# Two recurrences woven into an attention: the recurrence is handed out evenly up to the attention's last step instead of ending two steps ahead of it

## The chip, the cores and the metric

The kernel runs on one core of a Trainium2 chip. The metric is the device time of one execution in microseconds (us), less is better; several executions give a median. Beside the times there is one execution taken by the hardware profiler, with its trace. TensorE (PE) multiplies matrices, PEld is its loading of weights, VectorE (DVE), ScalarE (ACT) and GpSimd (POOL) do the rest of the arithmetic, and SyncE (SP) issues nearly all DMA transfers from one queue, in order.

## The reference

A trunk of two layers over 256 context rows and 2048 latent rows of width 1024, in float32. Each layer projects its input, runs two gated linear recurrences in both directions and one attention, and projects the three results together:

```python
h = layer_norm(x) * (1.0 + scale) + shift
(hq, hff, hfb, hi, hgate, mcq, mckv, mkr, mgate, gq, gk, gv, gaf, gab, ggate) = split_cols(h @ w_in)
...
hg_lat, hg_ctx = bidirectional_recurrence(hgrn2_inputs(...), ...)
gla_lat, gla_ctx = bidirectional_recurrence(gla_inputs(...), ...)
mla_lat = blockwise_attend(q, jnp.concatenate([k_c, k], axis=1), jnp.concatenate([v_c, v], axis=1))
y = jnp.concatenate([gated_head_norm(hg_lat, hg_norm_g, hgate),
                     mla_lat.reshape(B, N, MLA_W) * jax.nn.silu(mgate),
                     gated_head_norm(gla_lat, gla_norm_g, ggate)], axis=-1)
x_new = layer_norm(DEEPNORM_ALPHA * x + gate * (y @ w_out)) * ln_g + ln_b
```

The attention has 4 heads; every latent row looks at all 2304 rows. The recurrence, S_t = diag(exp(g_t)) S_(t-1) + k_t v_t and o_t = q_t S_t, is computed in chunks of 64 rows. The context rows run through everything in the first layer only.

## The kernel before, in words

A layer has three stages, one behind the other in the code: `project`, `mix` and `output`. Numbers are split into a high and a low part (`split`, lines 75 to 85: ScalarE rounds the high part at L79, VectorE subtracts at L85, or GpSimd at L83), and each product is three products of parts.

**The mixing stage, `mix`.** The attention works through groups of two tiles of 128 query rows. A tile has two steps, one for each pair of heads; so a group has four steps, and layer 1 has 8 groups and 32 steps. Layer 0 has 36, since a context group stands at the third place, whose steps see only the context. A step (`attend`) makes scores (`pss`, L905 to L909), scaled by VectorE into `sx` (L911), takes their maximum, lets ScalarE take the exponential in place (L924), transposes it on TensorE (`ptp`, L951), splits it into `ph` and `pl` (L79, L85), multiplies it with the compressed keys (`oc`, L938 and L943), copies that (`os`, L967), multiplies it with `uv` (`poa`, L970), and scales and gates it (`ym`, L974). Behind a tile's second step the rows `ym` are stored to `y` (L977); the gate's rows `mg` come by L892.

The recurrence works in 9 pairs of tiles. First come the states of the backward direction (`back_states`, one part for each pair, 1.0 units each), then for each pair ten parts of 0.25 units (`recur`): 31.5 units in all. A pair ends with `chunk_outputs`: products `po` on TensorE (L807, L818), `o` and its squares on ScalarE (L822, L825), their sums on VectorE (L827), a root and two multiplications on GpSimd (L90, L831, L832), and the store of `o` to `y` (L833).

Both are generators, and `mix` weaves them: before each attention step it writes as many parts of the recurrence as are due.

```python
total = self.npairs * 3.5
cost = [(self.CHEAP if t == 0 else 1.0) for t in order for _ in range(4)]
end = max(sum(cost) - self.LEAD, 1.0)
done, spent = 0.0, 0.0
for c in cost:
    spent += c
    while done < spent * total / end:
        ...
        done += w
    next(att, None)
```

With `LEAD` 2 the last part of the recurrence is written ahead of the last two steps. The order in the code is the priority of the instructions; a scheduler fixes from it, when the kernel is built, the order of the instructions of each engine and of SyncE's queue, and on the chip each runs in that order.

**The output stage, `output`.** Its tiles lie in memory that the pools of the mixing stage free. It loads the gate (L1058) and then w_out in eight pieces of 512 KB (`woraw`, L1066), each split into two `wo` (L79 and L83 for even pieces, L79 and L85 for odd ones); `lng` and `lnb` follow (L1073, L1074). The pieces have the tag "yt" with two buffers, and the same two buffers then hold the rows of `y` (`yt`, L1078). A tile of rows is transposed (`pty`, L1085), split into `yhl`, multiplied (`pzo`, L1105 to L1107), and then gated, added to the rows `xto` (L1098), normalized and stored (L1127) on the way over `z`.

**The next layer's weights.** While layer 0 ends, SyncE also loads the first input weights of layer 1 (`wraw`, L355, with three buffers; `wh` and `wl` are their split) and its `uv` (L260); they have a high priority.

Of the kernel before, what the change touches and what calls it, by code (L numbers as in the profile page):

```python
# [54 lines left out]
class Trunk:  # L55
# [923 lines left out]
    def mix(self, l, S):  # L979

        nc = self.nc
        with ExitStack() as ctx:
# [46 lines left out]
# [3 lines that stand above are left out]
# [96 lines left out]

    AHEAD = 600
    SOON = 300  # L1130
    LEAD = 2
    WHEN = 2
    CHEAP = 0.3
    EARLY = 1000
# [95 lines left out]
```

## Time and profile before

| | us |
|---|---|
| median of 2 runs | 3741.56 (3741.3 to 3741.82) |
| profiled execution, its own time | 3734.03 |
| its span in the trace | 3732.1 |
| PE busy in the span | 3597.6 (96%) |
| DVE, ACT, POOL busy | 2135.8, 1502.0, 810.8 |

The span runs from the first to the last instruction in the trace; the execution's own time has a little around it. Layer 0's mixing stage ends near 1722 us of the span and layer 1's near 3541. An engine counts as busy while it works on an instruction. An instruction's idle time before it is put down to the event that came last, its releaser.

### The profile page before, as it was taken

Reading aid. Unit: us, or ns where it says so; the run is one execution under the profiler, and the core shown is the slowest. Engines: PE = TensorE matmul, PEld = TensorE weight load, DVE = VectorE, ACT = ScalarE, POOL = GpSimd, SP = SyncE. Lnnn points to the kernel's source line nnn. Section 1 sums busy time; section 2 is a strip of 40 time slices with the busy share of each in tenths; the row PEclk is TensorE's granted clock in tenths of the full one; section 3 lists DMA queues with packets and bytes.
Section 4 is the critical chain, followed back from the end, with each engine's and each line's share of the span. In section 5 each row is a group of like instructions: output and inputs, shape, how many; then the busy total and the mean of one; then the engine's idle time right before and its main releaser. Section 6 shows DMA issues by size and latency. Waiting matters only on the chain. (4 is left out here: it accounts for less than half of the span.)

```text
span 3732.1 us, 85224 instructions
## 1 busy us (share of the span) xinstructions
PE 3597.6 (96%) x36056; PEld 3253.3 (87%) x36056; DVE 2135.8 (57%) x5162; ACT 1502.0 (40%) x2808; POOL 810.8 (22%) x617
## 2 busy tenths in 40 slices
PE   8899999999999999999999999999999999999899
PEld 5899999888888888887879999997888888888787
DVE  6764242466666666666765442425665566566566
ACT  3525242344454544453115252523444444544400
POOL 1000000001246454441110000000022344644211
PEclk9999999999999999999999999999999999999999
DMA  7774444322122122116435443533231122221332
GB/s 257 231 205 146 127 132 145 112 72 96 48 65 87 62 65 71 47 53 212 156 107 169 147 148 119 159 107 118 76 94 39 61 68 62 70 84 41 103 144 102
DMA packets 263693, 410.84 MB, mean 110 GB/s; under 512 B 39632, under 2 KB 179984, under 8 KB 262288
## 3 DMA queue, kind: packets, MB, share of 16 engines
q1 hardware_dynamic: 261872, 403.04, 33.9%
q8 instruction: 283, 4.64, 0.5%
q10 hardware_dynamic: 1440, 2.36, 0.2%
q14 instruction: 98, 0.80, 0.1%
HBM read 288.66 MB, written 116.67 MB: 109 GB/s over the span
## 5 line engine op out<-in xcount | busy, mean ns | idle before, releaser
L421 PE MATMUL pj<-wh,hl 128*128 128x256 f32 (+1 forms) x2224 | 622.1, 280 | 8.2 <-DVE hl L85 8.2
L421 PE MATMUL pj<-wh,hh 128*128 128x256 f32 (+1 forms) x2224 | 623.7, 281 | 1.6 <-DVE ve L373 1.4
L421 PE MATMUL pj<-wl,hh 128*128 128x256 f32 (+1 forms) x2224 | 622.7, 280 | 0.0
L911 DVE TENSOR_SCALAR_CACHE_REDUCE sx<-pss 128x512 f32<-128x512 f32 (+1 forms) x648 | 401.9, 631 | 199.9 <-PE pss L909 167.2
L85 DVE TENSOR_TENSOR pl<-ptp,ph 128x512 fp32r<-128x512 f32 x580 | 389.8, 687 | 154.2 <-ACT ph L79 146.6
L79 ACT CAST ph<-ptp 128x512 fp32r<-128x512 f32 x580 | 326.1, 584 | 292.0 <-PE ptp L951 273.4
L421 PEld LDWEIGHTS pj<-wh,hl 128*128 128x128 f32 x2224 | 420.0, 189 | 8.9 <-DVE hl L85 8.9
L421 PEld LDWEIGHTS pj<-wh,hh 128*128 128x128 f32 x2224 | 420.9, 189 | 2.0 <-DVE ve L373 1.6
L421 PEld LDWEIGHTS pj<-wl,hh 128*128 128x128 f32 x2224 | 420.8, 189 | 0.0
L924 ACT ACTIVATE sx<-sx,nm 128x768 f32<-128x768 f32 (+1 forms) x392 | 359.5, 920 | 147.5 <-DVE nm L917 145.9
L951 PE MATMUL ptp<-ident,sx 128*128 128x128 f32 x2320 | 365.6, 276 | 19.8 <-DVE pl L85 14.1
L938 PE MATMUL oc<-ph,cnh 128*128 128x256 f32 x1160 | 339.8, 316 | 35.7 <-ACT ph L79 35.6
L432 PE MATMUL pj<-hh,wh 128*128 128x256 f32 x1136 | 317.3, 279 | 0.0
L432 PE MATMUL pj<-hh,wl 128*128 128x256 f32 x1136 | 316.1, 278 | 0.0
L432 PE MATMUL pj<-hl,wh 128*128 128x256 f32 x1136 | 315.9, 278 | 0.0
L951 PEld LDWEIGHTS ptp<-ident,sx 128*128 128x128 f32 x2320 | 271.4, 141 | 41.2 <-DVE pl L85 17.0
L938 PE MATMUL oc<-ph,cnl 128*128 128x256 f32 x1160 | 302.0, 284 | 0.0
L85 DVE TENSOR_TENSOR wl<-wraw,wh 128x1024 fp32r<-128x1024 f32 (+1 forms) x144 | 169.5, 1211 | 226.4 <-ACT wh L79 226.4
L905 PE MATMUL pss<-cth,qh 128*128 128x512 f32 (+1 forms) x648 | 267.6, 413 | 15.3 <-DVE sx L911 15.2
L938 PEld LDWEIGHTS oc<-ph,cnh 128*128 128x128 f32 x1160 | 221.8, 191 | 65.9 <-ACT ph L79 53.2
L79 ACT CAST wh<-wraw 128x1024 fp32r<-128x1024 f32 (+1 forms) x144 | 142.5, 1039 | 246.3 <-PE pj L421 162.0
L907 PE MATMUL pss<-cth,ql 128*128 128x512 f32 (+1 forms) x648 | 241.3, 373 | 0.0
(254 smaller groups left out, 8023.7 us busy)
## 6 DMA issues: line engine op xcount, KB each, us to landing
wraw<-in_w_in_dram SPq DMA_DIRECT2D x132, 512.0 KB, 4.6
dnat<-stg SPq DMA_DIRECT2D x104, 256.0 KB, 2.1
vg<-dnat SPq DMA_DIRECT2D x17, 1024.0 KB, 6.1
yt<-dy SPq DMA_DIRECT2D x34, 512.0 KB, 3.7
wmt<-in_w_modT_dram SPq DMA_DIRECT2D x64, 256.0 KB, 4.1
fa<-dF SPq DMA_DIRECT2D x18, 768.0 KB, 4.2
ka<-dK SPq DMA_DIRECT2D x18, 768.0 KB, 4.2
dK<-stg SPq DMA_DIRECT2D x36, 256.0 KB, 4.4
```

What stands on the lines that cost most here:

```text
L79: nc.scalar.copy(hi, src)
L85: nc.vector.tensor_tensor(lo, src, hi, op=ALU.subtract)
L421: nc.tensor.matmul(pj[:, j, :n], h[pr][a][:, k, tk], w[b][:, k, :n], start=(k == 0 and a + b == 0), stop=(k == KD - 1 and a == 1))
L432: nc.tensor.matmul(pj[:, j, :], w[b][:, k, cs], h[pr][a][:, k, :], start=(k == 0 and a + b == 0), stop=(k == KD - 1 and b == 1))
L905: nc.tensor.matmul(pss[:, :n], G["qh"][hp][:, i, tk], K["cth"][:, ks], start=True, stop=False)
L907: nc.tensor.matmul(pss[:, :n], G["ql"][hp][:, i, tk], K["cth"][:, ks], start=False, stop=False)
L911: nc.vector.tensor_scalar(sx[:, ks], pss[:, :n], SCALE, None, op0=ALU.mult, op1=ALU.max, accum_out=mx[:, nb:nb + 1])
L924: nc.scalar.activation(sx[:, x0:x1], sx[:, x0:x1], AF.Exp, bias=nm, accum_out=s3[:, q:q + 1])
L938: nc.tensor.matmul(oc, K[k][:, keys(kc, c)], ph[:, c, :], start=(kc + c == 0 and k == "cnh"), stop=False)
L951: nc.tensor.transpose(pt[:, c, i, :], pexp[i][:, (kc + c) * P:(kc + c + 1) * P], self.ident)
```

## The change

The constant that tells how many steps ahead of the attention's end the recurrence is to be finished goes from 2 to 0.

```diff
     AHEAD = 600
     SOON = 300
-    LEAD = 2
+    LEAD = 0
     WHEN = 2
     CHEAP = 0.3
     EARLY = 1000
```

With that, `end` is the sum of the costs itself, and parts of the recurrence are due up to the last step. The instructions are the same in both kernels; their order changes through the whole of both mixing stages. The places at which the stages end are these.

SyncE's queue at the end of layer 1's mixing stage, before (`o` are rows of the recurrence, `ym` rows of the attention, `dy` is `y` in memory):

```order
L833 DMA dy_107<-o 128x2x512
L977 DMA dy_107<-ym 128x512
L892 DMA mg<-dnat_102 128x512
L1058 DMA gate<-gate_98 128x1024
L1066 DMA woraw<-in_w_out_dram 128x1024 x8
L1078 DMA yt<-dy_107 128x1024 x4
L1098 DMA xto<-xs_21645 128x1024 x2
L977 DMA dy_107<-ym 128x512
```

The same place after:

```order
L892 DMA mg<-dnat_102 128x512
L1098 DMA xto<-xs_21645 128x1024 x2
L977 DMA dy_107<-ym 128x512
L833 DMA dy_107<-o 128x2x512
L1058 DMA gate<-gate_98 128x1024
L1066 DMA woraw<-in_w_out_dram 128x1024 x2
L1073 DMA lng<-in_ln_g_dram 128x1024
L1074 DMA lnb<-in_ln_b_dram 128x1024
L1066 DMA woraw<-in_w_out_dram 128x1024 x6
L1078 DMA yt<-dy_107 128x1024 x5
```

The gate and w_out stood ahead of the last `ym` and now stand behind it and behind the last `o`; `lng` and `lnb` have come between the pieces of w_out.

SyncE's queue at the end of layer 0's mixing stage, before:

```order
L892 DMA mg<-dnat_90 128x512
L833 DMA dy_95<-o 128x2x512
L1058 DMA gate<-gate_86 128x1024
L1066 DMA woraw<-in_w_out_dram 128x1024 x6
L355 DMA wraw<-in_w_in_dram 128x4x224 x2
L355 DMA wraw<-in_w_in_dram 128x4x256
L1066 DMA woraw<-in_w_out_dram 128x1024 x2
L1078 DMA yt<-dy_95 128x1024 x3
```

The same place after:

```order
L260 DMA uv_24137<-in_uv_dram 128x512
L977 DMA dy_95<-ym 128x512
L355 DMA wraw<-in_w_in_dram 128x4x256 x2
L833 DMA dy_95<-o 128x2x512
L355 DMA wraw<-in_w_in_dram 128x4x256 x2
L1058 DMA gate<-gate_86 128x1024
L1066 DMA woraw<-in_w_out_dram 128x1024 x2
L1073 DMA lng<-in_ln_g_dram 128x1024
L1074 DMA lnb<-in_ln_b_dram 128x1024
L1066 DMA woraw<-in_w_out_dram 128x1024 x6
L1078 DMA yt<-dy_95 128x1024 x5
```

Here two pairs of the next layer's `wraw` stand ahead of the gate as well.

TensorE where layer 1's recurrence ends, after, with the rest of the attention's last step (repeating groups of `oc` and `ptp` left out in the middle are the same as those shown):

```order
L818 MATMUL po<-stf,qm 64x64 x8
L938 MATMUL oc<-ph,cnh 128x256
L938 MATMUL oc<-ph,cnl 128x256
L938 MATMUL oc<-ph,cnh 128x256
L938 MATMUL oc<-ph,cnl 128x256
L943 MATMUL oc<-pl,cnh 128x256 x2
L951 MATMUL ptp<-ident,sx 128x128 x4
...
L943 MATMUL oc<-pl,cnh 128x256 x4
L970 MATMUL poa<-uv_24137,os 128x128 x2
L1085 MATMUL pty<-ident,yt 128x128 x8
L1105 MATMUL pzo<-wo,yhl 128x512
```

Before, the last `po` had the rest of a step and two whole steps behind it; in front of the last `poa` stood products `pzo` of the output stage.

## Rows read from the trace of the kernel before

**Rows 1.** The page, part 1: busy us (share of the span) and instructions of each engine.
```profile
PE 3597.6 (96%) x36056; PEld 3253.3 (87%) x36056; DVE 2135.8 (57%) x5162; ACT 1502.0 (40%) x2808; POOL 810.8 (22%) x617
```

**Rows 2.** Windows: stretch, us, busy us (x) of PE, PEld, DVE, ACT, POOL; PEclk, DMA share, GB/s.
```profile
1605.00:1663.86 58.86, 58.67 (x973) 51.79 (x973) 36.81 (x95) 28.12 (x57) 31.91 (x23) 1.00 0.12 38
1663.86:1722.46 58.60, 51.41 (x331) 45.79 (x331) 38.02 (x79) 34.92 (x58) 16.73 (x7) 0.94 0.49 164
3473.40:3536.40 63.00, 54.69 (x351) 48.66 (x351) 34.28 (x77) 32.64 (x55) 16.70 (x7) 0.95 0.39 126
730.00:1663.86 933.86, 898.53 (x11544) 789.21 (x11542) 592.68 (x1622) 451.50 (x900) 343.96 (x242) 0.99 0.21 65
2575.00:3473.40 898.40, 869.25 (x10773) 758.74 (x10771) 564.33 (x1562) 431.61 (x859) 313.40 (x228) 1.00 0.21 65
1706.00:1708.00 2.00, 2.00 (x11) 2.00 (x10) 1.05 (x2) 0.92 (x2) 0.00 (x0) 0.50 0.81 277
```

**Rows 3.** Timeline of PE: start, us, instruction, [idle before, releaser]; the long waits.
```profile
1699.53 0.88 PE L951 MATMUL ptp<-ident,sx 128*128 128x128 f32 x6 [2.49 <-ACT sx L924]
1702.78 0.58 PE L938 MATMUL oc<-ph,cnh 128*128 128x256 f32 x1 [2.38 <-ACT ph L79]
...
3513.13 0.88 PE L951 MATMUL ptp<-ident,sx 128*128 128x128 f32 x6 [2.52 <-ACT sx L924]
3516.59 0.58 PE L938 MATMUL oc<-ph,cnh 128*128 128x256 f32 x1 [2.58 <-ACT ph L79]
```

**Rows 4.** Timeline of SyncE's queue, layer 0, then layer 1 (SPq: its DMA issues).
```profile
1675.54 0.39 SPq L833 DMA_DIRECT2D dy<-o  x1
...
1676.53 20.50 SPq L1066 DMA_DIRECT2D woraw<-in_w_out_dram  x6
...
3484.97 0.36 SPq L833 DMA_DIRECT2D dy<-o  x1
...
3487.49 26.27 SPq L1066 DMA_DIRECT2D woraw<-in_w_out_dram  x8
3518.52 13.04 SPq L1078 DMA_DIRECT2D yt<-dy  x4
```

**Rows 5.** The chain of waits through layer 1: start, us, what.
```profile
3497.39 3.48 DMA woraw<-in_w_out_dram
...
3500.89 1.05 ACT wo L79
...
3502.02 2.40 POOL wo L83
```

**Rows 6.** Timeline of PE, layer 0, from the recurrence's last product on.
```profile
1663.80 0.39 PE L938 MATMUL oc<-ph,cnh 128*128 128x256 f32 x1
...
1670.09 0.39 PE L905 MATMUL pss<-cth,qh 128*128 128x512 f32 x1
...
1672.38 0.40 PE L943 MATMUL oc<-pl,cnh 128*128 128x256 f32 x2
...
1673.31 0.64 PE L970 MATMUL poa<-uv,os 128*128 128x128 f32 x4
```

**Rows 7.** Timeline of PE, layer 1: the first transposes and the first output product.
```profile
3522.10 1.09 PE L1085 MATMUL pty<-ident,yt 128*128 128x128 f32 x8
...
3524.88 0.40 PE L1105 MATMUL pzo<-wo,yhl 128*128 128x512 f32 x1
```

**Rows 8.** Lines by form: xcount | busy us, mean ns of one | idle before, releaser.
```profile
L85 DVE TENSOR_TENSOR wl<-wraw,wh 128x1024 fp32r<-128x1024 f32 x132 | 157.0, 1222 | 166.7 <-ACT wh L79 166.6
...
L974 DVE SCALAR_TENSOR_TENSOR ym<-poa,ri,mg 128x128 f32<-128x128 f32 x136 | 41.4, 346 | 27.8 <-PE poa L970 25.8 <-DMA mg<-dnat 0.9
```

**Rows 9.** DMA issues: xcount, KB each, median us from issue to landing.
```profile
wraw<-in_w_in_dram SPq DMA_DIRECT2D x132, 512.0 KB, 4.6
...
lng<-in_ln_g_dram SPq DMA_DIRECT2D x2, 512.0 KB, 8.4
```

**Rows 10.** Waits of PE in layer 0's mixing stage, 730 to 1663.86 us: total, times, longest.
```profile
PE oc L938 <- ACT ph L79: 15.2, 19, 2.7
```

## The prediction, made before the changed kernel ran

> **What bounds the kernel now.** I read the page first. TensorE is busy 96% of the span [rows 1], so a stretch matters only if TensorE stands still in it, and the question is how still it stands where the recurrence ends, the attention goes on alone and the output's weights are fetched. The windows answer that [rows 2]. While the recurrence is woven in, TensorE is busy 58.67 of 58.86 us just ahead of its last product in layer 0. From that product to the last product of the attention it is busy 51.41 of 58.60 us, and in layer 1 54.69 of 63.00 us: 7.2 and 8.3 us of standstill. These 15.5 us are all that the change can win there. Over the rest of the two mixing stages TensorE stands still 933.86 - 898.53 = 35.3 us and 898.40 - 869.25 = 29.2 us.
>
> The timeline of TensorE shows where the 15.5 us lie: in the last step but one of the stage, two waits of 2.5 and 2.4 us for the exponentials and for the first cast of them, in layer 1 2.5 and 2.6 us [rows 3]. Behind them the clock is at half: a granted clock of 0.50, the level of 1.2 GHz, still at 1706 to 1708 us [rows 2].
>
> The third view is SyncE's timeline [rows 4], for what else happens in those 60 us. After the recurrence's last product the store of its rows is issued 11.7 us later (1663.86 to 1675.54; layer 1: 3473.40 to 3484.97, 11.6), because the o, its squares, three GpSimd operations and a reduction stand between. Right behind it in the same queue come the gate and the eight loads of w_out. The chain of waits through layer 1 shows what these then cost: it runs load (3.48 us), cast on ScalarE (1.05), subtraction on GpSimd (2.40) and again load [rows 5]. The loads have two buffers, and these are the buffers of the rows of y too, so from the first load's issue to the first yt's issue it takes 3518.52 - 3487.49 = 31.0 us [rows 4]. In the kernel before, this chain runs beside the last two attention steps and TensorE computes all the while.
>
> **The change part by part.**
>
> *What moves.* The recurrence costs 31.5 units in both kernels; the attention's steps sum to 33.2 in layer 0 (the context group counts 0.3 a step) and 32 in layer 1. Before, 31.5 / 31.2 = 1.01 and 31.5 / 30 = 1.05 units go to a step, after it 31.5 / 33.2 = 0.95 and 31.5 / 32 = 0.98. No instruction is added or taken away. The order rows show the result: the last po now stands in the last attention step, with only a few groups of oc and ptp and one poa behind it, and on SyncE the store of o, the gate and all w_out loads now come behind the last store of ym.
>
> *The end of the attention, called E.* Behind the last po five groups of oc and ptp and the poa are left. Before, the same work ran from 1663.80 to 1673.95 us with ten score products (1670.09 to 1672.38, 2.3 us) in it [rows 6], so E is 10.15 - 2.3 = 7.9 us behind the last po. The recurrence's tail still takes 11.6 us, so its store is issued at E + 3.7, and the first w_out load 1.0 us later (1675.54 to 1676.53 [rows 4]), at E + 4.7.
>
> *Layer 1.* The 31.0 us of the chain follow: the first yt is issued at E + 35.7. From a yt's issue to the first pzo it was 3524.88 - 3518.52 = 6.4 us before, with attention products in between; the transposes began 3.6 us after the issue and took 1.1 us [rows 4, 7]. I take 5.5: first pzo at E + 41.2. Of this TensorE works 1.1 us; it stands still 40.1 us. What covered the chain before was the attention, and that is gone: nothing else is left for TensorE to do.
>
> *Layer 0.* Here SyncE also carries the next layer's first input weights, and the order rows put two pairs of wraw between the last ym and the gate. Each pair waits for the buffer that a split frees. ym is issued at E + 0.8 (two of 346 ns [rows 8]); the subtraction that frees the first buffer ends near E + 1.8, a load lands 4.6 us after its issue [rows 9], and cast and subtraction take 1.05 (as the cast in [rows 5]) and 1.2 us [rows 8], so the last wraw goes out near E + 8.8. The gate follows, and the first w_out load at E + 9.6 instead of E + 4.7. First pzo at E + 46.1, standstill 45.0 us.
>
> *The clock.* After the two waits TensorE worked at half clock from 1702.78 us [rows 3] to at least 1708 [rows 2], some 5 to 6 us, of which half, up to 3 us, are lost; since TensorE would partly have waited for ScalarE and VectorE in it, I take 2.4. Before there is one in each layer (4.8); after it one behind each long standstill (4.8), and with a chance of a half each the old one stays (2.4).
>
> *What remains of the standstill before.* The last step's exponentials still have to be waited for (2.5 + 2.4 us), with little of the recurrence behind which to hide them; I count on 1.3 us of filling from it: 3.6 us a layer, 7.2 in all.
>
> *The sum.* 40.1 + 45.0 + 4.8 = 89.9 us added; 15.5 + 4.8 = 20.3 us taken away; 7.2 + 2.4 = 9.6 us kept: 89.9 - 20.3 + 9.6 = +79.2 us. The profiled execution took 3734.03 us (its span was 3732.1), so the changed kernel's would take 3813. The median of the runs, 3741.56, is 7.5 us above that execution; on it the time is 3741.56 + 79.2 = **3821 us**, 2.1% more.
>
> How much a filled stretch wins could be judged otherwise than by the busy time of products. Loads of weights were busy 51.79 of 58.86 us where TensorE was filled, 88%, and 45.79 of 58.60 us behind it [rows 2]. The Trainium skill (Perfetto Trace Analysis, Identifying the Most-Contended Engine) holds that the busy time of matmuls, being pipelined, tells little of how near TensorE is to its limit, and that the busy share of weight loads does. By that the change could win 58.6 x 0.88 - 45.79 = 5.8 and 63.0 x 0.88 - 48.66 = 6.8 us in place of 7.2 and 8.3, and the sum would be some 3 us higher.
>
> **The rivals.**
>
> *Not slower: the thinner recurrence pays for it.* With 5 to 6% less of the recurrence at each step, TensorE would wait less often for ScalarE's cast ph (15.2 us of the 35.3 in layer 0's stage [rows 10]) since that engine serves both strands. Place: the two stages ahead of the tail, with 64.5 us of standstill. The point from which it decides is low: 2% is 74.8 us, so 5 us back put the time within it. Against it: recurrence and attention each keep the same work, most waits are of one attention strand on itself, and thinner filling can lengthen them as well as shorten them. A third of it back, 21 us, gives 3800; all of it 3756. The Trainium skill (Perfetto Trace Analysis, Optimization Strategy) says that interleaving regimes with different bounds may improve a kernel. That speaks for this rival; the trace supports it in the filled stretch (58.67 of 58.86 us), but the exposed chain is a regime that it no longer interleaves.
>
> *Slower still: the loads go slower.* The order rows put lng and lnb, two loads of 8.4 us to land [rows 9], between the first two and the next six w_out loads. If the third load lies behind their transfers, up to 8 us come on top in each layer: +95, 3837. Against it: the third waits for GpSimd anyway, 7 us after the first. Nor is it sure that the queue waits as I lined it up in layer 0, where several buffers are in question; that is worth up to 5 us more or less.
>
> *It comes out even or ahead because the chain starts earlier.* If the w_out loads did not wait for the recurrence's tail, 11 us of each standstill would go: 3799. Only SyncE's order decides that, and in both layers the store of o stands ahead.
>
> **How the numbers follow.** Forecast 0.53; not slower by thinner filling 0.28; loads slower still 0.14; an earlier chain 0.05. A measurement of this kernel can tell about 2% from no change, 74.8 us or 3816. The forecast's own spread, about 12 us, crosses that bound, so of its 0.53 about 0.06 falls within 2%; with the 0.33 of the others, less a little, within 2% gets 0.36 and slower 0.62. Faster by 2% would need more than the 64.5 + 15.5 us of standstill and none of the chain: 0.02. The range goes from 3785, where half of the standstill of the stages comes back, to 3846, with both loads' delays and 9 us more in layer 0.
>
> **What would show it.** In the changed profile: in each layer one standstill of TensorE of 40 to 45 us between the last poa and the first pzo, with only eight transposes in it; w_out loads issued 4 to 10 us after the last poa; GpSimd subtractions of w_out with a period of 7 us while TensorE is idle; half clock behind the standstill. The standstill of the stages ahead would stay near 35 and 29 us. I am wrong if the loads start ahead of the last poa, if the chain takes much less than 31 us now that nothing else uses the queue, or if the stages ahead become shorter by more than 10 us.

## The result, and the profile after

The changed kernel takes 3843.43 us (median of 2 runs, 3841.74 to 3845.12), 101.9 us more than the 3741.56 us of the kernel before; the ratio is 1.0273, 95% interval 1.0257 to 1.0290. The forecast was 3821 us, between 3785 and 3846. The profiled execution is the one of 3841.74 us; it is 107.7 us longer than the profiled one of before (3734.03), which lay 7.5 us below its median, and the spans differ by 107.8 us. The engines on the page of the changed kernel:

```profile
PE 3625.3 (94%) x36056; PEld 3266.0 (85%) x36056; DVE 2159.8 (56%) x5162; ACT 1508.1 (39%) x2808; POOL 813.3 (21%) x617
```

Beside [rows 1], TensorE is busy 27.7 us longer, with the same 36056 products, and stands still for 214.6 us in place of 134.5. Where it stands still, its waits over the whole span say (total, times, longest):

```profile
PE pty L1085 <- DMA yt<-dy: 84.9, 2, 45.8
```

A wait that was in no view of before takes 84.9 us in two pieces: the first transposes of the output stage wait for the rows of y. The timeline of TensorE at the end of the two mixing stages:

```profile
1728.02 0.71 PE L970 MATMUL poa<-uv,os 128*128 128x128 f32 x4 [0.46 <-ACT os L967]
1774.51 1.97 PE L1085 MATMUL pty<-ident,yt 128*128 128x128 f32 x8 [45.77 <-DMA yt<-dy]
1776.30 0.79 PE L1105 MATMUL pzo<-wo,yhl 128*128 128x512 f32 x1
```

```profile
3596.42 0.71 PE L970 MATMUL poa<-uv,os 128*128 128x128 f32 x4 [0.46 <-ACT os L967]
3636.22 1.97 PE L1085 MATMUL pty<-ident,yt 128*128 128x128 f32 x8 [39.08 <-DMA yt<-dy]
3638.01 0.80 PE L1105 MATMUL pzo<-wo,yhl 128*128 128x512 f32 x1
```

Behind the last poa come 45.8 us of nothing in layer 0 and 39.1 us in layer 1, and then the transposes and the first pzo. In layer 1 these rows answer to [rows 7], where the same transposes stood among products of the attention. SyncE's queue in layer 0, for the whole of that standstill:

```profile
1730.96 3.53 SPq L355 DMA_DIRECT2D wraw<-in_w_in_dram  x2
1734.54 0.50 SPq L833 DMA_DIRECT2D dy<-o  x1
1735.25 3.21 SPq L355 DMA_DIRECT2D wraw<-in_w_in_dram  x2
1738.51 0.49 SPq L1058 DMA_DIRECT2D gate<-gate  x1
1739.05 0.90 SPq L1066 DMA_DIRECT2D woraw<-in_w_out_dram  x2
1739.99 0.82 SPq L1073 DMA_DIRECT2D lng<-in_ln_g_dram  x1
...
1749.96 15.70 SPq L1066 DMA_DIRECT2D woraw<-in_w_out_dram  x6
1770.96 5.86 SPq L1078 DMA_DIRECT2D yt<-dy  x3
```

and in layer 1:

```profile
3600.84 0.37 SPq L833 DMA_DIRECT2D dy<-o  x1
...
3601.77 1.33 SPq L1066 DMA_DIRECT2D woraw<-in_w_out_dram  x2
3604.41 0.33 SPq L1073 DMA_DIRECT2D lng<-in_ln_g_dram  x1
...
3611.72 15.34 SPq L1066 DMA_DIRECT2D woraw<-in_w_out_dram  x6
3632.59 5.95 SPq L1078 DMA_DIRECT2D yt<-dy  x3
```

Beside [rows 4]: the last poa ends at 1728.73 (1728.02 and 0.71) and 3597.13 us. The store of o comes 5.8 and 3.7 us behind that, the first piece of w_out 10.3 and 4.6 us, and the first rows of y 31.9 and 30.8 us behind the first piece. Two pairs of wraw fill the difference in layer 0. Between the second and the third piece stand lng and lnb, but it is not they that hold the third: it goes out at 1749.96, when the first subtraction ends (1747.59 and 2.35, below), and that is 10.9 us behind the first piece, in layer 1 9.9; before it was 12.0 and 9.9. GpSimd's timeline shows the rest of the chain in layer 0, one subtraction after every second load:

```profile
1747.59 2.35 POOL L83 TENSOR_TENSOR wo<-woraw,wo 128x1024 fp32r<-128x1024 f32 x1 [14.45 <-ACT wo L79]
1754.57 2.34 POOL L83 TENSOR_TENSOR wo<-woraw,wo 128x1024 fp32r<-128x1024 f32 x1 [4.63 <-ACT wo L79]
...
1768.60 2.34 POOL L83 TENSOR_TENSOR wo<-woraw,wo 128x1024 fp32r<-128x1024 f32 x1 [4.66 <-ACT wo L79]
```

The period is 7.0 us. In layer 1 before, with TensorE and the other engines at work beside it, it was 7.0 to 7.1 (subtractions at 3494.99, 3502.02, 3509.06 and 3516.13 us); in layer 0 before, where three loads of wraw stood between the pieces, one of the three periods was 9.1. So the chain is bound by its own links. While TensorE stands, its clock falls, and the windows show that it comes back late (columns as in [rows 2]):

```profile
1728.73:1774.51 45.78, 0.01 (x2) 0.00 (x1) 13.72 (x11) 11.27 (x12) 13.70 (x6) 0.55 0.69 230
1774.51:1776.50 1.99, 1.99 (x9) 1.77 (x10) 0.22 (x1) 0.59 (x1) 0.00 (x0) 0.50 0.58 224
1778.50:1781.00 2.50, 2.50 (x12) 2.01 (x12) 0.69 (x1) 0.59 (x1) 0.00 (x0) 1.00 0.27 107
```

The eight transposes run at half clock, 1.2 GHz, and take 1.97 us instead of 1.09; by 1778.5 us the clock is full again. In layer 1 it takes longer: the granted clock is 0.50 from the transposes at 3636.22 on, still 0.50 at 3639 to 3641 us, and 1.00 at 3641.3 to 3643.3, with TensorE busy in all of it.

The rest of the loss lies in the mixing stages themselves. The stages by windows of TensorE (from the first scores to the end of the last poa; stretch, us, PE busy, PEclk, DMA share, GB/s), before:

```profile
698.20:1722.46 1024.26, 975.47 (x12107) 0.99 0.25 77
2546.80:3541.75 994.95, 952.77 (x11362) 0.99 0.24 75
```

and after:

```profile
700.90:1728.73 1027.83, 983.31 (x12078) 0.99 0.23 69
2604.50:3597.13 992.63, 948.99 (x11298) 0.99 0.22 66
```

The stretch before holds some products of the output stage too: 5.3 us of them in layer 0 and 12.9 in layer 1, added up from TensorE's rows. Without them the mixing stages' own products kept TensorE busy for 970.2 and 939.9 us, and now for 983.3 and 949.0: 13.1 and 9.1 us more for the same instructions, together 22 us, at a granted clock of 0.99 in all four stretches. The standstill inside the stages goes from 48.8 and 42.2 us to 44.5 and 43.6.

So the 107.8 us of the two spans divide thus: 84.9 the two standstills, about 22 longer busy time in the mixing stages, -2.9 standstill within them, 2.7 a later start of the first stage (698.2 to 700.9 us, ahead of all that changed) and 1 us for the rest. (The 18.2 us of output products that ran inside the stages now run behind them; that moves time from one place to another and adds none.)

### The profile page after: what moved, and what is told of

Same layout as the page of the kernel before. It is cut to its first block, busy times and chain, and to the rows that moved or that the text cites. A ratio compares the mean times of both kernels' runs of the same rounds, so it can differ in the third digit from the quotient of the medians.

```text
span 3839.9 us, 85190 instructions
## 1 busy us (share of the span) xinstructions
PE 3625.3 (94%) x36056; PEld 3266.0 (85%) x36056; DVE 2159.8 (56%) x5162; ACT 1508.1 (39%) x2808; POOL 813.3 (21%) x617
## 5 line engine op out<-in xcount | busy, mean ns | idle before, releaser
L938 PE MATMUL oc<-ph,cnh 128*128 128x256 f32 x1160 | 337.5, 314 | 25.1 <-ACT ph L79 23.5
L951 PEld LDWEIGHTS ptp<-ident,sx 128*128 128x128 f32 x2320 | 268.8, 141 | 38.6 <-DVE pl L85 15.5
L908 PE MATMUL pss<-ks,rh 128*128 128x512 f32 (+1 forms) x648 | 241.8, 373 | 0.7 <-ACT rh L79 0.7
```

The lines of the kernel that those rows point to most:

```text
L908: nc.tensor.matmul(pss[:, :n], G["rh"][j][:, h, :], K["ks"][:, ks], start=False, stop=False)
L938: nc.tensor.matmul(oc, K[k][:, keys(kc, c)], ph[:, c, :], start=(kc + c == 0 and k == "cnh"), stop=False)
L951: nc.tensor.transpose(pt[:, c, i, :], pexp[i][:, (kc + c) * P:(kc + c + 1) * P], self.ident)
```

## The experiments

**What was to be told apart.** The first theory has two parts. *Exposure*: 85 us are the chain of w_out's loads and splits, which nothing covers any more. *Passages*: the 22 us come from the finer weave. Each time TensorE goes from the attention's products, which use its whole array, to the recurrence's small ones (po, pa and pu, on 64 rows) and back, it loses time. Counted in the traces, it goes over to the small ones 153 and 157 times in the two stages before, and 184 and 186 times after. Against both stood the *pace*: that a thinner recurrence costs time throughout; and for the 22 us alone the *half clock*. What a passage costs can be seen in part in rows of the kernel before (layer 1, TensorE):

```profile
3441.76 0.39 PE L943 MATMUL oc<-pl,cnh 128*128 128x256 f32 x2
3441.99 0.60 PE L951 MATMUL ptp<-ident,sx 128*128 128x128 f32 x4
...
3443.03 0.39 PE L943 MATMUL oc<-pl,cnh 128*128 128x256 f32 x2
3443.35 1.77 PE L789 MATMUL pa<-qa,km 64*64 64x64 f32 x64
3445.05 0.66 PE L951 MATMUL ptp<-ident,sx 128*128 128x128 f32 x4
```

Two oc at 3441.76 are followed by ptp 0.23 us later; the same two at 3443.03 by pa 0.32 us later. Averaged one by one over layer 1's stage before, where TensorE did not wait, an oc of L943 is followed by ptp after 122 ns and by pa after 212, a pa by a pa after 27 ns and by ptp after 156. From start to start, a passage there and back so costs some (212 - 122) + (156 - 27) = 219 ns at its two seams.

That is not the whole of it, since busy time is counted by ends: a product adds the time from the end of the one before it (or from its own start, if TensorE stood still) to its own end, as the profile models the ends. By ends the same four averages are 119, 207, 26 and 267 ns, and the passage costs (207 - 119) + (267 - 26) = 329 ns. Over all products of the two stages before, a full-array product behind another adds 149 ns, a small one behind a small one 22, a small one behind a full-array one 203 and a full-array one behind a small one 316: 203 + 316 - 149 - 22 = 348 ns for a passage, and 320 to 360 for single pairs of kinds. After the change the four are 149, 22, 204 and 319, which makes 352 ns. With the counts that is 310 x 0.348 = 107.9 us before and 370 x 0.352 = 130.2 after: 22.3 us more, the whole of the 22. A change between two kinds of full-array products has no such price: a ptp adds 119 ns behind an oc and 111 behind another ptp.

**Own buffers for w_out**, in the changed kernel:

```diff
-R = Route(lambda: self.pool(ctx), "yt", "woa", ...
+R = Route(lambda: self.pool(ctx), "yt", "woraw", "woa", ...
-w = R.tile([P, D], F32, tag="yt", bufs=2, name="woraw")
+w = R.tile([P, D], F32, tag="woraw", bufs=4, name="woraw")
```

> The changed kernel, but the pieces of w_out get four buffers of their own instead of sharing two with the rows of y. Exposure theory (85 of the 102 us are the chain of w_out loads and splits that stands alone behind the attention's last poa): the first four pieces go out together and the rows of y no longer wait for the last split, so the two standstills of 46 and 39 us fall to 15 to 25 us each, and the time to about 3800 (3785 to 3812). Rival (the thinner pace through the whole of both stages costs the time, the standstill is only where it shows): it stays within 10 us of the changed kernel, above 3830.

It took 3818.03 us, 25 us less than the changed kernel (ratio to before 1.0205, 1.0188 to 1.0222). Its SyncE queue in layer 1, and the waits of TensorE over the whole span:

```profile
3604.45 2.59 SPq L1066 DMA_DIRECT2D woraw<-in_w_out_dram  x4
3607.09 0.96 SPq L1078 DMA_DIRECT2D yt<-dy  x2
3614.20 4.71 SPq L1066 DMA_DIRECT2D woraw<-in_w_out_dram  x4
```

```profile
PE pty L1085 <- DMA yt<-dy: 32.1, 2, 16.3
...
PE pt L383 <- DVE xt L375: 15.2, 2, 12.7
```

Four pieces go out together and two rows of y right behind them. From the last poa to the first pzo it is now 18.1 and 17.6 us where it was 47.6 and 40.9. That part came as the exposure theory has it, and with the pace unchanged. Only half of these 53 us is in the time: layer 1's part is there in full, but in layer 0 the way from the first pzo to the second mixing stage took 852 us in place of 828. Layer 1's first transposes (`pt`) now wait for xt, 12.7 us in one piece, and TensorE's order is another there: in the changed kernel the first of them stand among layer 0's last output products, here all stand behind them. And the mixing stages were 11 us busier. The upper limit given was 3812, so the size was missed.

**One step ahead.**

```diff
-    LEAD = 2
+    LEAD = 1
```

> The recurrence ends one step ahead of the attention's last. Exposure theory: a step of some 28 us covers more than half of tail, chain and first rows (11.6 + 1 + 31.0 + 5.5 = 49 us from the last po on), so TensorE stands still some 12 to 20 us a layer, and the time is 3765 to 3785. Rival (the cost goes with the pace): half of the change's cost, 3785 to 3800.

3791.26 us (1.0140, 1.0125 to 1.0155), above the exposure theory's range and within the rival's. The trace says what the total does not:

```profile
PE pty L1085 <- DMA yt<-dy: 41.8, 2, 22.5
```

The wait for the rows of y is back, half as long, in a kernel that ends the recurrence 31 us ahead of the last poa. The first pzo comes 24.3 and 21.1 us behind that poa. I had expected 12 to 20: six pieces go out ahead of the last store of ym and only the last two behind it. The busy time of the stages is 7.7 us above before and their standstill 6.3 us. Of the 56.9 us between the two profiled spans (3789.0 and 3732.1) the wait of 41.8 us is thus by far the largest part, so the chain is again most of the loss, though the time alone would not tell the theories apart.

**Lumps of a whole pair**, in the kernel before, behind the back states:

```diff
-while done < spent * total / end:
+due = spent * total / end
+while done < due and (done < 9 or due - done >= 2.5 or (done - 9) % 2.5 or due >= total):
```

> The kernel before (ends two steps ahead), but behind the back states the recurrence is handed out in lumps of a whole pair (2.5 units) instead of parts of 0.25; nothing is exposed at the end, and by the instruction order TensorE passes from full-array products to the small 64-row products of the recurrence 469 times instead of 310 (370 in the changed kernel). Switch theory (the 22 us by which the same products keep TensorE busy for longer in the changed kernel come from such passages, 0.3 to 0.4 us each): TensorE's busy time grows by 40 to 65 us, time 3780 to 3810. Rival (passages are free, the 22 us come from stretches at half clock): busy time within 10 us of before, and the time differs only by idle time.

3806.97 us (1.0182, 1.0167 to 1.0197). The page:

```profile
PE 3667.1 (96%) x36056; PEld 3281.6 (86%) x36056; DVE 2151.9 (57%) x5162; ACT 1507.7 (40%) x2808; POOL 813.1 (21%) x617
```

69.5 us more of busy time than [rows 1] with the same products, a little over the upper end of the 40 to 65 that were expected; the standstill of the span is 137.9 us against 134.5, and there is no wait for rows of y. The 469 passages are 159 more than before: 0.42 us each by the stages' busy time (1977.1 against 1910.2 us). The mean granted clock is 0.989 against 0.990, so the half clock is ruled out as the cause.

**Four steps ahead** (e4_lead4).

```diff
-    LEAD = 2
+    LEAD = 4
```

> The recurrence ends four steps ahead of the attention's last. Exposure theory: the chain was covered already with two steps, nothing is won by more; two more steps of attention alone, which stands still 4 to 5 us in each where softmax is waited for, less what pzo fills: 3745 to 3760. Rival (a quicker pace is what helps): below 3735.

3767.42 us (1.0072, 1.0057 to 1.0087): slower than either theory said. That the chain was covered already is borne out: no wait for rows of y is left. The passages are 180 and 149, and the busy time of layer 0's stage is 14.4 us above before (both stages: 11.7). In addition TensorE waits 12.4 us for VectorE's z in the output stage, which starts earlier now and is interrupted by the attention's last steps; neither had been counted.

**1.75 steps ahead.**

```diff
-    LEAD = 2
+    LEAD = 1.75
```

> The recurrence ends 1.75 steps ahead of the attention's end: nearly the pace of the kernel before, and by the instruction order the first rows of y still stand ahead of the attention's last store, so nothing of the chain is exposed. But TensorE passes from the attention's products to the small products of the recurrence 202 and 183 times in the two stages, against 153 and 157 before. Switch theory (0.3 to 0.47 us for each passage more): TensorE's busy time in the stages grows by 22 to 35 us, time 3760 to 3780. Rival (the thinner pace itself costs, in proportion to the units a step): a tenth of the change's 102 us or less, below 3750.

3773.34 us (1.0088, 1.0072 to 1.0103), as the passages have it: busy time of the stages 1941.9 us, 31.7 more than before with 75 more passages, 0.42 each; their standstill is 9.9 us longer as well. The pace is nearly that of before. This speaks against the pace as a cause.

**Whole units** (e6_whole2), in the kernel before:

```diff
-while done < spent * total / end:
+due = spent * total / end
+while done < due and (due - done >= 1 or done % 1 or due >= total):
```

> The kernel before (two steps ahead), with the recurrence handed out in whole units (four parts of 0.25 at a time); by the instruction order 134 and 147 passages instead of 153 and 157, nothing exposed. Switch theory: busy time of the two stages falls by 9 to 14 us, time 3725 to 3733, a better kernel than both. Rival (passages are free): 3735 to 3745.

3728.96 us, a ratio of 0.9971 to before (0.9961 to 0.9981): 11.8 us faster than the kernel before and better than both.

```profile
PE 3590.1 (96%) x36056; PEld 3250.5 (87%) x36056; DVE 2147.4 (58%) x5162; ACT 1503.2 (40%) x2808; POOL 812.0 (22%) x617
```

7.5 us less busy time than before on the page, 8.7 in the stages, for 29 fewer passages.

**Whole units in the changed kernel** (the same edit, on `LEAD = 0`).

> The changed kernel, with the recurrence handed out in whole units: the same end of the stages as in the changed kernel, with the loads of w_out behind the last store of ym, but 167 and 151 passages instead of 184 and 186. Exposure and switch theories together: the standstills of 46 and 39 us stay, busy time of the stages falls by 16 to 24 us, time 3818 to 3828. If passages are free it stays at 3838 to 3848; if the exposure came from the fine parts, the standstills shrink.

3846.72 us (1.0285, 1.0271 to 1.0299): a miss. The passages did fall to 318 and the busy time of the stages by 13.3 us, 0.26 each, but the standstill in the stages rose by 11.3 us (44.5 to 53.5 and 43.6 to 45.9), and the wait for the rows of y stayed, 89.4 us. Fewer passages are longer stretches of one kind, in which TensorE waits more for the other engines: its waits for ScalarE's cast ph ahead of oc went from 23.5 us in the two stages to 35.4. In this order that ate the gain.

**Whole units, and VectorE for all low parts of w_out**, on the kernel before:

```diff
-self.split(wh[k], wl[k], w, lo_eng="dve" if k % 2 else "pool")
+self.split(wh[k], wl[k], w, lo_eng="dve")
```

> As e6_whole2, and all low parts of w_out are subtracted on VectorE instead of every second one on GpSimd: the chain's period falls from 7.0 to about 5.9 us, so the chain ends some 4 us sooner and the first output products can fill part of the 2.5 us waits for the exponentials of the last step but one. Exposure theory: 0 to 8 us less than e6_whole2. Rival (VectorE, which also scales and splits for the last attention steps, becomes late): the same or up to 10 us more.

3740.27 us, the same as before (0.9996, 0.9987 to 1.0005), 11.3 us above the whole units alone. The busy time of the stages is the same (1901.4 us), and the output's products did fill more of the attention's end. On the pages TensorE is 5.6 us busier over the whole span (3595.7 against 3590.1) and stands still 4.7 us longer; why was not followed.

**Whole units four and three steps ahead** (the same edit, on `LEAD = 4` and `LEAD = 3`).

> The recurrence ends four steps ahead (as e4_lead4, 3767 us), handed out in whole units: 125 and 132 passages by the instruction order, against 180 and 149 in e4_lead4 and 153 and 157 in the kernel before. Switch theory (0.38 to 0.40 us for a passage): busy time of the stages 25 to 33 us below e4_lead4's, time 3730 to 3745. Rival (what costs in e4_lead4 is the quicker pace or the four steps of attention alone): above 3755.

> The recurrence ends three steps ahead, in whole units: 142 and 138 passages, nothing exposed. Switch theory: busy time of the stages 9 to 14 us below the kernel before, time 3724 to 3736. Rival (passages are free): 3738 or more.

3747.14 us (1.0012, 1.0003 to 1.0021) and 3759.48 us (1.0042, 1.0029 to 1.0054). The first, just above its range, took 20.3 us from the 3767.42 with the same four steps (by their ratios to before, 0.6%, 22 us): the stages are 24.0 us less busy for 72 fewer passages. The second missed: its stages were 10.4 us less busy than before, as expected, but the standstill in them was 8.4 us longer, and 11.4 us went in waits for z in the output stage, which I had left out for more than two steps.

**The store of the last o from ScalarE's queue**, in the changed kernel:

```diff
-nc.sync.dma_start(out=self.pair_rows(S["y"], p, 0, 512), in_=o)
+(nc.scalar if p == self.npairs - 1 else nc.sync).dma_start(out=self.pair_rows(S["y"], p, 0, 512), in_=o)
```

> The changed kernel, but the last pair's store of o is issued from ScalarE's queue, so that SyncE's queue no longer waits for the recurrence's tail ahead of the gate and w_out; their order is otherwise the same. If SyncE's order holds the loads back: in layer 1 the first w_out load goes out 1 to 2 us behind the last poa instead of 4.6, the standstill of 39 us falls by 2 to 4 us; in layer 0, where two pairs of wraw also stand ahead of the gate, by 0 to 2 us; time 3836 to 3844. If the memory of w_out's buffers holds them back, nothing moves.

3845.65 us (1.0271, 1.0257 to 1.0285), no change. In layer 1 (last poa ends at 3596.89):

```profile
3597.57 0.32 SPq L977 DMA_DIRECT2D dy<-ym  x1
...
3598.46 0.88 SPq L1066 DMA_DIRECT2D woraw<-in_w_out_dram  x2
3609.02 0.33 SPq L1073 DMA_DIRECT2D lng<-in_ln_g_dram  x1
...
3610.21 17.79 SPq L1066 DMA_DIRECT2D woraw<-in_w_out_dram  x6
```

The first two pieces go out 1.6 us behind the last poa in place of 4.6, so SyncE's order did hold them back. But lng now stands in the queue until 3609.02, and the third piece goes out 11.8 us behind the first in place of 9.9; the wait for the rows of y is 40.5 us. What lng waits for can be read in the trace: it is the landing of that same store of o, which goes out at 3600.59 and lands at 3608.87, and SyncE's waits put 9.5 us of lng's down to it. In the changed kernel too lng goes out right behind that landing (3604.34 and 3604.41). So the store had left the queue, but not the chain. In layer 0 the first piece goes out 10.2 us behind the last poa, as in the changed kernel: there the four wraw stand ahead of it.

**All traces together.** The number of passages and the busy time of the mixing stages' own products, both added up from TensorE's rows in thirteen traces (residual: distance from the line below; counted product by product, which puts the changed kernel 0.5 us under the 983.3 + 949.0 of its windows):

```
                    passages  busy us   residual
before                  310    1910.2     -3.4
after                   370    1931.8     -5.0
own buffers             371    1943.0     +5.8
one step ahead          314    1917.9     +2.8
lumps of a pair         469    1977.1     +2.2
four steps ahead        329    1921.9     +1.0
1.75 steps ahead        385    1941.9     -0.7
whole units             281    1901.5     -0.9
whole, changed          318    1918.5     +1.8
whole, VectorE          282    1901.4     -1.4
whole, four steps       257    1897.9     +4.7
whole, three steps      280    1899.8     -2.3
o from ScalarE          370    1932.1     -4.7
```

A straight line through them has 0.39 us for each passage, with no point farther from it than 5.8 us. What was varied is the order of the instructions, not the passage alone, so the line by itself is only a strong bond over 80 us of busy time. The seams go farther: added up by ends as above, a passage costs 346 to 356 ns in every one of the thirteen traces. Passages times price account for 22 of the 22 us in the changed kernel, 59 of the 67 with lumps, 26 of the 32 with 1.75 steps, 24 of the 33 with own buffers, and 11 for the 9 us less with whole units. What lies beside them, up to 9 us, was not followed. The Trainium skill (TensorEngine Tiling (Array Packing), Key Properties) says that changing the tiling mode drains TensorE. The runs agree in so far as each passage between the full array and the small products costs 0.35 us; that it is a drain no row tells.

## Why the prediction was right, and where it was too small

*The end of the attention and the tail.* From the last po to the end of the last poa I had 7.9 us; it is 7.8 in both layers. The first piece of w_out behind that was to come after 9.6 us in layer 0 and 4.7 in layer 1; it came after 10.3 and 4.6.

*The chain.* 31.0 us from first piece to first yt became 31.9 and 30.8, and the standstills of 45.0 and 40.1 us became 45.8 and 39.1. Both right. The 31.0 had been read in layer 1; in layer 0 it was 35.4 before (1676.53 to 1711.96), with three loads of wraw in it, which now stand ahead of the chain, so that layer 1's figure served for both. The rival of slower loads did not come about: the third piece waited for the subtraction and not for lng and lnb, though not 7 us behind the first but 10.9 and 9.9, the same as before or less. The measured time lies nearer to that rival's 3837 than to the 3821, by another cause.

*The clock behind the standstill* was right in kind: half clock with TensorE busy for some 3 us in layer 0 and 5 in layer 1, of which half at most is lost, 1.5 and 2.5 us where I took 2.4 each.

*The standstill inside the stages* was to fall by 15.5 - 7.2 = 8.3 us; it fell by 2.9. (Layer 1's stretch in [rows 2] ends 5.5 us ahead of the last poa at 3541.92; TensorE was busy in all of these, so the 8.3 us stand.)

*The term that failed* is the one that is not in the sum: the step "No instruction is added or taken away", with the mixing stages priced by their standstill alone. The same instructions in another order kept TensorE busy for 22 us longer, because the small products of the recurrence now came in 370 groups instead of 310. With this term the sum is 79.2 + 22 = 101, against 101.9 between the medians; that it fits so closely is in part luck, since the two profiled executions, from which the terms are read, are 107.7 us apart: the standstill in the stages fell by 5.4 us less than forecast, and 2.7 us are the later start. The rival that hoped for a gain from a thinner weave looked in the right place with the wrong sign. It was also wrong that the pace decides: the groups number 314, 370, 385, 310 and 329 for 1, 0, 1.75, 2 and 4 steps, so it is what the scheduler makes of the weave, and it could have been counted in the two orders ahead of any run; the price of a passage could have been read from the seams in the trace of before.

That the loads' exposure and not the pace makes the 85 us is shown by three runs: with own buffers at the same pace the gap to the first pzo fell from 47.6 and 40.9 to 18.1 and 17.6 us; with the recurrence 31 us ahead it was 24.3 and 21.1; with 1.75 steps there was none, the first pzo came ahead of the last poa. Freeing the gap did not win the same in time, though: with own buffers about half of the 53 us were lost again elsewhere.

## What to carry to other kernels

When the last part of one strand is moved up to the end of another, ask first what was running under the work that is no longer left behind it: here a chain of loads and splits of 31 us, bound by two buffers, and a queue that serves in order. Where two strands share TensorE, count how often it goes from one's products to the other's in the finished order; the same work in fewer and longer groups is shorter, as long as no engine waits for it.

## What the hardware showed that was not expected

A passage from full-array products to 64-row products and back cost 0.35 us of TensorE's busy time at its seams, the same within 3% in thirteen orders with 257 to 469 passages. Counted from start to start on one pair of groups it had looked like 0.22 us. And the chain of loads and splits kept its period of 7.0 us in layer 1 whether TensorE worked beside it or not.
